# Block products in the first feed-forward as well, with w2 parts and modulation columns re-routed

## Chip, core and metric

One Trainium2 chip, and on it one core. The metric is the device time of one execution in microseconds (us); several executions are taken and their median is given.

## The reference, cut to what matters

A two-layer backbone over 512 tokens of width 1024 with 256 context tokens. Layer 0 mixes with a 2-D Fourier transform and windowed attention, layer 1 with a pooling mixer; each layer ends with a SwiGLU feed-forward of hidden width 2816. Every sub-layer is normed and modulated by shift, scale and gate columns that come from the condition `c`.

```python
def ada_mod(cond, w, b):
    m = jax.nn.silu(cond) @ w + b
    return jnp.split(m[..., None, :], 6, axis=-1)
def swiglu(h, w1, w3, w2):
    return (jax.nn.silu(h @ w1) * (h @ w3)) @ w2
...
    for layer in range(DEPTH):
        sh1, sc1, g1, sh2, sc2, g2 = ada_mod(c, ada_w[layer], ada_b[layer])
        ...
        h = h + g1 * y
        hn = modulate(rms_norm(h, norm_ffn_g[layer]), sh2, sc2)
        h = h + g2 * swiglu(hn, ffn_w1[layer], ffn_w3[layer], ffn_w2[layer])
    return rms_norm(h, final_g)
```

All of it is float32.

## The kernel before

**Layout and precision.** The stream `h` lies transposed in SBUF: 128 partitions by 8 blocks (`kt`) by 512 tokens. A float32 product is made of three TensorE passes over a high and a low part (`passes`, lines 181 to 185): w_h with the high part of the moving operand, w_l with the high part, w_h with the low part. So each weight and each activation is split first: the high part is a copy into the shorter format on ACT (`act`, line 68), the low part is source minus high part on VectorE (line 153).

**The feed-forward (`ffn`, line 1018).** The 2816 hidden channels are 22 tiles of 128, in three groups of 8, 8 and 6 (`GROUPS`). First come the normed inputs: `norm_apply` makes for each kt an `nrm_u` (VectorE, line 360), its high part `hnh` (ACT) and its low part `hnl` (VectorE, line 366). For each hidden tile, w1 and w3 products go into PSUM, `si` is the silu of the one (ACT), `av` the product with the other (VectorE), `ah` and `al` its parts. After a group come eight w2 products (`w2_ps`, one for each dt), which VectorE adds to h (line 1083) scaled by the gate column.

A *direct* tile has 48 matmuls 128x512: for each kt three passes of w1 and three of w3. Tile 0 is the *lead* (`Lead`): its product runs on the stream before the norm is known, with correction by a shift (`wb`, `sh_ps`, `z`). A *quartered* tile (`Quarters`, line 903) makes the same two products from 2x2 blocks with seven block products instead of eight (the scheme of Strassen and Winograd): 7 x 4 x 3 = 84 matmuls 128x256. For it the inputs are combined once per layer (`pieces`: `t_f` and its parts t_h, t_l on VectorE and ACT, four of them, t1 to t4), the weights of every tile are combined (`prepare`: `s_f`, four VectorE operations of 512, then split into w_h and w_l), and the outputs are combined after the products (`run`: x, y, c_q, three to five small operations). The parts of the two uncombined weights come by `low`: ACT writes the high part and its negative, and a DMA from POOL's queue adds the weight from DRAM to that negative (line 941). In `run` the products come in the order b11, t1, t2, b21, t3, b22, t4; the first use of each result bank waits until its last reader is through. `QUARTERED` says which tiles of which layer: none of layer 0, 4 to 21 of layer 1.

**Weight stream (`Stream`).** `ws` holds all units (w1, w3, w2 parts) in order of use. SP's queue loads them raw, 512 KB each, into four rotating buffers; `split` fills rotating slots for w_h and w_l, two units ahead of use.

**Modulation columns (`AdaCols`).** A `step` is one load of 512 KB (`ada_r`) and one VectorE operation over 128x1024 with an accumulator (line 222), which gives 128 columns' worth of `silu(c) @ w`. `acol1` has 88 steps; those that remain when layer 0's feed-forward begins go there, three after each tile from tile 2 on (the program's condition `l == 0 and j > 1`), and share the raw buffers with the weights.

**What sets the order.** Each engine runs its queue in order. The program is written in a natural order and a scheduler orders each engine's queue by its own estimates; `pinned` ties an instruction to its place behind the last one written for its engine; in a layer with quartered tiles PE keeps the written order (`manual_schedule`). SBUF is shared out by pools; a tile in a reused place waits for the last user of that place.

Of the kernel before, what the change touches and what calls it, by code (L numbers as in the profile page):

```python
# [16 lines left out]
P = 128  # L17
# [6 lines left out]
QUARTERED = (frozenset(), frozenset(range(4, NHID)))  # L24
NA = 17
# [6 lines left out]
def kernel(  # L32
# [47 lines left out]
    def f32(ap):  # L80
        return ap.bitcast(F32)
# [4 lines left out]
    def pick(pool, tag):  # L86
        return pb if tag == "tmp" else pool

# [37 lines left out]
    class Stream:  # L126


        def __init__(self, units, LD=4, LS=2):
            self.units, self.LD, self.LS, self.raw, self.ready, self.used = units, LD, LS, [], [], 0  # L130
            self.whole, self.slots = {i for i, u in enumerate(units) if len(u) > 2}, 0
# [23 lines left out]

        def slots_for(self, n):
            pool, t = (wp_, "") if alt["pool"] is None or self.slots % 2 == 0 else (alt["pool"], "2")
            self.slots += 1
            return [pool.tile([P, n], F32R, tag=w + t, bufs=3, name=m) for w, m in (("whi", "w_h"), ("wlo", "w_l"))]
# [44 lines left out]
    class AdaCols:  # L204


        def __init__(self, blocks):
            self.tasks = [(l, t) for l, t0 in blocks for t in range(t0, t0 + 8)]
            self.raw, self.done = [], 0

        def load(self, n):
            while len(self.raw) < min(n, len(self.tasks)):
                l, t = self.tasks[len(self.raw)]
                self.raw.append(raw_tile(1024, "ada_r"))
                nc.sync.dma_start(out=self.raw[-1], in_=adaR[48 * l + t])

        def step(self, ahead=1):
# [10 lines left out]
            self.load(self.done + ahead)  # L228

    class Norm:  # L230
# [7 lines left out]
        def add(self, kt, src):  # L238
            sq, n = self.sq, self.n
            tag, bufs = sq[:2] if kt else sq[2:]  # L240
            s = pick(self.pool, tag).tile([P, n], F32, tag=tag, bufs=bufs, name="sq")
# [136 lines left out]
    def ffn_units(l):  # L378
        u = []
        for gi, (j0, nj) in enumerate(GROUPS):  # L380
            for j in range(j0, j0 + nj):
                whole = (True,) if j in QUARTERED[l] else ()
                u += [(w1[l, j], 1024) + whole, (w3[l, j], 1024) + whole]
            u += [(w2a[l, gi, dt] if gi < 2 else w2b[l, dt], nj * P) for dt in range(KT)]
        return u
# [8 lines left out]
    with ExitStack() as es:  # L394
# [3 lines left out]
        def sl(name, n=512, dt=F32, tag="tmp", bufs=8):  # L398
            return pick(pt, tag).tile([P, n], dt, tag=tag, bufs=bufs, name=name)
# [494 lines left out]
    pq = stage.enter_context(tc.tile_pool(name="pq", bufs=1))  # L894
# [3 lines left out]
    def sf(name, n=512, dt=F32, tag="tmp", bufs=8):  # L898
        return pick(pf, tag).tile([P, n], dt, tag=tag, bufs=bufs, name=name)
# [3 lines left out]
    class Quarters:  # L903
# [79 lines left out]
        def run(self, left):  # L983
# [4 lines left out]
            x, y, si = sf("x"), sf("y"), sf("si")  # L988
            c = self.pool.tile([P, 768], F32, tag="c", bufs=1, name="c_q")
            q0, q1, q2 = [slice(256 * q, 256 * q + 256) for q in range(3)]  # L990
# [13 lines left out]
            nc.vector.tensor_tensor(c[:, q2], y[:, q0], r[3], op=ALU.add)  # L1004
# [5 lines left out]
            nc.vector.tensor_tensor(c[:, q0], x[:, q1], r[2], op=ALU.add)  # L1010
            act(si[:, q1], c[:, q0], AF.Silu)
            self.product(r[3], w["a22"], 0, "t4")
            nc.vector.tensor_tensor(c[:, q1], x[:, q1], r[3], op=ALU.add)
            av = sf("av")
            nc.vector.tensor_tensor(av, si, c[:, 256:768], op=ALU.mult)
            return av

    def ffn(l, rstd, A, lead, each=None, pool=None):
        nonlocal ss
        nrm = Norm(pf, T)  # L1020
# [17 lines left out]
        for gi, (j0, nj) in enumerate(GROUPS):  # L1038
            a = []
            for j in range(j0, j0 + nj):  # L1040
# [30 lines left out]
                if l == 0 and j > 1:  # L1071
                    for _ in range(3):
                        acol1.step()
            for dt in range(KT):
# [5 lines left out]
                for j in range(nj):  # L1080
# [3 lines left out]
                                               in1=h[:, dt, :], op0=ALU.mult, op1=ALU.add)  # L1084
                if gi == len(GROUPS) - 1:
# [10 lines left out]
    bh = pq.tile([P, 4, 536], F32R, tag="bh", bufs=1, name="bh")  # L1096
    bl = pq.tile([P, 4, 40], F32R, tag="bl", bufs=1, name="bl")
# [36 lines left out]
    nrm = ffn(0, rstd, Af, lead, pool_in)  # L1134
# [66 lines left out]
    with tc.tile_pool(name="pt8", bufs=1, reuse_waits="tile") as pt8:  # L1201
        rstd = ffn(1, rstd, Af1, lead, pool=pt8).rstd_short()
# [107 lines left out]
```

## Time and profile before

| | |
|---|---|
| median of 3 runs | 996.86 us (995.17 to 997.55) |
| the profiled execution | 996.72 us, of which the span of the profile is 995.0 us |
| granted TensorE clock | 0.994 |
| busy: PE, VectorE (DVE), ACT, POOL | 962.3, 665.6, 450.6, 58.5 us |
| layer 0's feed-forward, from its second tile on | 252.4 to 601.6 us, PE 348.82 of 349.20 busy |
| HBM read | 150.41 MB |

Rows of the profile name line, engine, operation, output and inputs with shapes. In rows of groups, "xN | busy, mean ns | idle before" gives the count, the summed time, the mean of one and the engine's idle time just ahead of them with what ended it. In rows of single instructions the first number is the start in us and the second the duration. Line L68 is the helper `act`, so ACT rows are told apart by their tiles.

### The profile page before, as it was taken

The page shows a single profiled execution, that of the slowest core. Times are in us where ns is not written, and L with a number is a line of the kernel's source. Part 1 is how long each engine was busy: PE and PEld are TensorE (multiplying, and loading weights), DVE is VectorE, ACT ScalarE, POOL GpSimd, SP SyncE. Part 2 cuts the span into 40 slices and gives each one's busy share as a digit, 9 for nine tenths or more (in the row PEclk, how much of TensorE's full clock was granted, in tenths as well). Part 3 has the DMA queues.
Part 4 walks back from the last instruction along what each step waited for, and adds up shares of the span by engine and source line. Part 5 has one row for each costly group of instructions (what it writes and reads, how often), then busy time and mean ns, then how long its engine had stood idle before and what let it go on. Part 6 is the DMA issues. An engine that isn't in the chain of part 4 may idle for free.

```text
span 995.0 us, 14007 instructions
## 1 busy us (share of the span) xinstructions
PE 962.3 (97%) x5464; PEld 804.6 (81%) x5464; DVE 665.6 (67%) x1086; ACT 450.6 (45%) x707; POOL 58.5 (6%) x63
## 2 busy tenths in 40 slices
PE   5999999998999999999999999999999999999995
PEld 3767777776888888888888888789988999889984
DVE  4678677879966546655365388998645776458644
ACT  4467666445632212223122365675533765337531
POOL 1011011002000000000000001000010110101100
PEclk9999999999999999999999999999999999999998
DMA  9931211653576546665366333136652786527602
GB/s 338 345 106 32 106 44 65 217 189 119 178 267 239 187 134 219 223 225 193 106 212 200 118 108 127 33 74 181 180 149 64 184 187 176 153 64 174 150 17 85
DMA packets 49602, 153.43 MB, mean 154 GB/s; under 512 B 6016, under 2 KB 6144, under 8 KB 49536
## 3 DMA queue, kind: packets, MB, share of 16 engines
q1 hardware_dynamic: 44352, 138.38, 41.1%
q0 software_dynamic: 5184, 14.16, 8.4%
q8 instruction: 43, 0.70, 0.3%
q14 instruction: 23, 0.19, 0.1%
HBM read 150.41 MB, written 2.10 MB: 153 GB/s over the span
## 4 chain that ended last, share of the span: by engine, by line
PE 89%; DVE 6%; ACT 3%; issue 2%; DMA 0%; DVEq 0%; SPq 0%; ACTq 0%
PE h_ps L183 15%; PE h_ps L184 15%; PE h_ps L185 15%; PE w_ps L184 8%; PE w_ps L183 8%; PE w_ps L185 8%; PE pv_ps L769 2%; PE t_ps L758 2%; PE mo_ps L183 1%; PE mo_ps L185 1%; PE mo_ps L184 1%; ACT w_h L68 1%; PE s_ps L721 1%; PE s_cx L434 1%; DVE w_l L153 1%
## 5 line engine op out<-in xcount | busy, mean ns | idle before, releaser
L68 ACT ACTIVATE w_h<-w_r 128x1024 fp32r<-128x1024 f32 (+2 forms) x158 | 148.7, 943 | 255.1 <-PE h_ps L185 115.8
L184 PE MATMUL h_ps<-hnh,w_l 128*128 128x512 f32 (+1 forms) x600 | 210.8, 351 | 0.4 <-DVE w_l L153 0.4
L183 PE MATMUL h_ps<-hnh,w_h 128*128 128x512 f32 (+1 forms) x600 | 210.9, 351 | 0.0
L185 PE MATMUL h_ps<-hnl,w_h 128*128 128x512 f32 (+1 forms) x600 | 210.7, 351 | 0.0
L153 DVE TENSOR_TENSOR w_l<-w_r,w_h 128x1024 fp32r<-128x1024 f32 (+2 forms) x122 | 137.1, 1126 | 33.6 <-ACT w_h L68 33.2
L222 DVE SCALAR_TENSOR_TENSOR ada_r<-ada_r,condB 128x1024 f32<-128x1024 f32 x80 | 97.6, 1222 | 70.2 <-DMA ada_r<-in_adaR_dram 70.1
L183 PE MATMUL w_ps<-ah,w_h 128*128 128x512 f32 x352 | 137.0, 389 | 0.0
L184 PE MATMUL w_ps<-ah,w_l 128*128 128x512 f32 x352 | 137.0, 389 | 0.0
L185 PE MATMUL w_ps<-al,w_h 128*128 128x512 f32 x352 | 137.0, 389 | 0.0
L184 PEld LDWEIGHTS h_ps<-hnh,w_l 128*128 128x128 f32 x600 | 113.6, 189 | 15.7 <-DVE w_l L153 0.8
L183 PEld LDWEIGHTS h_ps<-hnh,w_h 128*128 128x128 f32 x600 | 113.6, 189 | 15.1
L185 PEld LDWEIGHTS h_ps<-hnl,w_h 128*128 128x128 f32 x600 | 113.6, 189 | 14.9
L1083 DVE SCALAR_TENSOR_TENSOR h<-w_ps,ada,h 128x512 f32<-128x512 f32 x48 | 36.0, 750 | 91.2 <-PE w_ps L185 91.2
L183 PE MATMUL h_ps<-t_h,w_h 128*128 128x256 f32 x288 | 82.3, 286 | 1.4 <-DVE av L1060 0.9
L185 PE MATMUL h_ps<-t_l,w_h 128*128 128x256 f32 x288 | 81.6, 283 | 0.0
L184 PE MATMUL h_ps<-t_h,w_l 128*128 128x256 f32 x288 | 81.5, 283 | 0.0
L185 PEld LDWEIGHTS w_ps<-al,w_h 128*128 128x128 f32 x352 | 66.1, 188 | 13.8
L183 PEld LDWEIGHTS w_ps<-ah,w_h 128*128 128x128 f32 x352 | 66.1, 188 | 13.7
L184 PEld LDWEIGHTS w_ps<-ah,w_l 128*128 128x128 f32 x352 | 66.1, 188 | 13.4
L68 ACT ACTIVATE w_h<-s_f 128x1024 fp32r<-128x1024 f32 x36 | 38.2, 1060 | 60.5 <-PE w_ps L185 30.7
L183 PEld LDWEIGHTS h_ps<-t_h,w_h 128*128 128x128 f32 x288 | 55.2, 192 | 2.6 <-DVE c_q L1004 1.4
L184 PEld LDWEIGHTS h_ps<-t_h,w_l 128*128 128x128 f32 x288 | 55.3, 192 | 0.0
(274 smaller groups left out, 1543.9 us busy)
## 6 DMA issues: line engine op xcount, KB each, us to landing
w_r<-in_w_dram SPq DMA_DIRECT2D x88, 512.0 KB, 4.1
ada_r<-in_adaR_dram SPq DMA_DIRECT2D x80, 512.0 KB, 4.2
w_r<-in_w2a_dram SPq DMA_DIRECT2D x32, 512.0 KB, 4.4
w_l<-in_w_dram POOLq DMA_DIRECT2D x18, 512.0 KB, 5.9
ada_q<-in_adaP_dram SPq DMA_DIRECT2D x32, 256.0 KB, 5.7
w_r<-in_w2b_dram SPq DMA_DIRECT2D x16, 384.0 KB, 3.1
w_l<-in_w_dram POOLq DMA_DIRECT2D x18, 256.0 KB, 6.0
w_r<-in_wo_dram SPq DMA_DIRECT2D x16, 256.0 KB, 2.8
```

What stands on the lines that cost most here:

```text
L68: return nc.scalar.activation(out=out, in_=in_, func=func, **kw)
L153: nc.vector.tensor_tensor(lo, src, f32(hi), op=ALU.subtract)
L183: nc.tensor.matmul(acc, wh, mh, start=start, stop=False, skip_group_check=shared)
L184: nc.tensor.matmul(acc, wl, mh, start=False, stop=False, skip_group_check=shared)
L185: nc.tensor.matmul(acc, wh, ml, start=False, stop=stop, skip_group_check=shared)
L222: nc.vector.scalar_tensor_tensor(out=r, in0=r, scalar=1.0, in1=condB, op0=ALU.mult, op1=ALU.mult, accum_out=ada[l][:, t:t + 1])
L434: nc.tensor.matmul(ps[32 * g:32 * g + 32, :], condS[:, kt, :], r[:, k * n:(k + 1) * n], start=(kt < 4), stop=(kt >= 4), tile_position=(0, ...
L721: nc.tensor.matmul(sp[:, c:c + n], q, KH[kv][:, k0:k0 + n], start=True, stop=False)
L758: nc.tensor.transpose(tp[:, c * P:(c + 1) * P], Ps[c][:, n * P:(n + 1) * P], ident)
L769: nc.tensor.matmul(ops[64 * kv:64 * kv + 64, 0:256], VS[:, kbs[n], kv, :], th[:, 256 * kv:256 * kv + 256], start=(n == 0), stop=(n == N - ...
L1083: nc.vector.scalar_tensor_tensor(out=h[:, dt, :], in0=acc, scalar=ada[l][:, 40 + dt:41 + dt], in1=h[:, dt, :], op0=ALU.mult, op1=ALU.add)
```

## The change

`QUARTERED` gets the tiles 6 to 21 of layer 0 as well. Round it, memory and work are moved:

- The remaining columns: two steps after each of tiles 1 to 5 of layer 0 in the shared raw buffers; from then on two buffers of their own ("adar"), one step after each quartered tile and 11 in each w2 stage of groups 0 and 1; the last eight in layer 1's first tiles. All are pinned on VectorE.
- The w2 units of layer 0 ("alone") are no longer loaded and split: POOL's queue loads the high part itself, ACT writes its negative into the low part's place, POOL's queue adds the weight to that (`by_dma`). They are filled three units ahead instead of two.
- The temporaries of the pool `pb` go to `pt` and `pf` (six instead of eight in `pf`), `NA` is 16 instead of 17, `c_q` takes a temporary of 512, and the pool that holds the combined inputs is opened inside `ffn`, for both layers. The buffers of the pooling stage are opened ahead of the last w2 stage of layer 0.

```diff
-QUARTERED = (frozenset(), frozenset(range(4, NHID)))
-NA = 17
+QUARTERED = (frozenset(range(6, NHID)), frozenset(range(4, NHID)))
+NA = 16
...
+                if len(self.raw) in self.alone:
+                    self.raw.append(None)
+                    continue
...
-            while len(self.ready) < min(used + self.LS, len(self.units)):
+            while len(self.ready) < len(self.units):
                 k = len(self.ready)
-                if k in self.whole:
+                if k in self.whole or k >= used + self.LS + (k in self.alone):
                     break
                 self.load(k + 1)
-                self.ready.append(self.split(self.raw[k]))
+                self.ready.append(self.split(self.raw[k]) if k not in self.alone else self.by_dma(self.units[k]))
...
+        def by_dma(self, unit):
+            hi, lo = self.slots_for(unit[1])
+            nc.gpsimd.dma_start(out=hi, in_=unit[0])
+            act(lo, f32(hi), scale=-1.0)
+            nc.gpsimd.dma_start(out=lo, in_=unit[0], accum_op=ALU.add)
+            return hi, lo
...
-                self.raw.append(raw_tile(1024, "ada_r"))
+                self.raw.append(pf.tile([P, 1024], F32, tag="adar", bufs=2, name="ada_r") if self.alone
+                                else raw_tile(1024, "ada_r"))
...
-            u = pb.tile([P, n], F32, tag="tmp", bufs=8, name="nrm_u")
+            u = pool.tile([P, n], F32, tag="tmp", bufs=8, name="nrm_u")
...
-    def sf(name, n=512, dt=F32, tag="tmp", bufs=8):
-        return pick(pf, tag).tile([P, n], dt, tag=tag, bufs=bufs, name=name)
+    def sf(name, n=512, dt=F32, tag="tmp", bufs=6):
+        return pf.tile([P, n], dt, tag=tag, bufs=bufs, name=name)
...
-            c = self.pool.tile([P, 768], F32, tag="c", bufs=1, name="c_q")
+            x, y, si, c = sf("x"), sf("y"), sf("si"), sf("c_q")
...
-    def ffn(l, rstd, A, lead, each=None, pool=None):
+    def ffn(l, rstd, A, lead, each=None, then=None):
+        phase = ExitStack()
+        pool = phase.enter_context(tc.tile_pool(name="pt8", bufs=1, reuse_waits="tile"))
...
-                if l == 0 and j > 1:
-                    for _ in range(3):
-                        acol1.step()
+                if j > 0:
+                    acol1.alone = l == 1 or j + 1 >= quartered[0]
+                    for _ in range(2 if (j == 6 if l else j < quartered[0]) else 1):
+                        if l or acol1.done < 48:
+                            pinned(DVE, acol1.step)
+            if gi == len(GROUPS) - 1:
+                phase.close()
+                if then:
+                    then()
...
+                if l == 0 and gi < 2:
+                    for n in range(2 if dt % 3 == 2 or dt == 0 else 1):
+                        pinned(DVE, acol1.step)
```

Where the order of the queues moves, first VectorE at the start of layer 0's feed-forward, before (`wb` belongs to the lead, `nrm_u` and `hnl` to the normed inputs):

```order
L153 TENSOR_TENSOR w_l<-w_r,w_h 128x1024
L315 SCALAR_TENSOR_TENSOR wb<-w_r,ada_106,wb 128x128
L360 SCALAR_TENSOR_TENSOR nrm_u<-h,Af_2364,bc_ps 128x512
L315 SCALAR_TENSOR_TENSOR wb<-w_r,ada_106,wb 128x128
L360 SCALAR_TENSOR_TENSOR nrm_u<-h,Af_2364,bc_ps 128x512
L315 SCALAR_TENSOR_TENSOR wb<-w_r,ada_106,wb 128x128
L366 SCALAR_TENSOR_TENSOR hnl<-nrm_u,ada_106,hnh 128x512
```

The first two nrm_u stand between the last wb. The same place on VectorE after the change:

```order
L163 TENSOR_TENSOR w_l<-w_r,w_h 128x1024
L326 SCALAR_TENSOR_TENSOR wb<-w_r,ada_106,wb 128x128 x3
L371 SCALAR_TENSOR_TENSOR nrm_u<-h,Af_2364,bc_ps 128x512
L163 TENSOR_TENSOR w_l<-w_r,w_h 128x1024
L371 SCALAR_TENSOR_TENSOR nrm_u<-h,Af_2364,bc_ps 128x512
L377 SCALAR_TENSOR_TENSOR hnl<-nrm_u,ada_106,hnh 128x512
```

All wb now stand ahead of the first nrm_u, which in the built program waits for the last `sh_ps` matmul, the end of the lead product; sixteen norm operations follow it.

VectorE after the change from tile 3's last column steps to tile 5's av (`s_f` are the combined weights of the tiles 6 and 7; the second av is tile 5's):

```order
L233 SCALAR_TENSOR_TENSOR ada_r,ada_106<-ada_r,condB 128x1024 x2
L163 TENSOR_TENSOR w_l<-w_r,w_h 128x1024
L963 TENSOR_TENSOR s_f<-w_r 128x512
L968 TENSOR_TENSOR s_f<-w_r 128x512
L1072 TENSOR_TENSOR av<-si,h_ps 128x512
...
L163 TENSOR_TENSOR w_l<-s_f,w_h 128x1024
L233 SCALAR_TENSOR_TENSOR ada_r,ada_107<-ada_r,condB 128x1024 x2
L963 TENSOR_TENSOR s_f<-w_r 128x512
L968 TENSOR_TENSOR s_f<-w_r 128x512
L1072 TENSOR_TENSOR av<-si,h_ps 128x512
```

Before, such av had only w_l and column steps around them; now the column steps and s_f of the quartered tiles stand ahead of both av. In SP's queue the raw loads of tile 6 wait for the buffers that the two steps of the first row read.

ACT after the change, from the x of group 0's last tile (tile 7) to that tile's ah; `w_l<-w_h` of 1024 are the negatives of w2 parts, each behind a plain transfer of POOL's queue:

```order
L68 ACTIVATE x<-h_ps 128x256
L68 ACTIVATE w_l<-w_h 128x1024
L68 ACTIVATE si<-h_ps 128x256
L68 ACTIVATE w_l<-w_h 128x1024
L68 ACTIVATE si<-y 128x256
L68 ACTIVATE w_l<-w_h 128x1024
L68 ACTIVATE w_h<-w_r 128x512
L68 ACTIVATE ah<-av 128x512
```

Three such passes stand ahead of the ah that the w2 products need, where before the ACT queue had splits of loaded weights (`w_h<-w_r`) between si and ah. Two more stand ahead of the x of that tile.

More of the change, by code (lines that the diff above doesn't have):

```diff
@@ L84, in big @@
         return pb.tile([P, 4, T], F32R, tag="b8", bufs=4, name=name)
-    def pick(pool, tag):
-        return pb if tag == "tmp" else pool
     cond_sb = cp.tile([P, KT, 2], F32, name="cond_sb")
@@ L130, in __init__ @@
             self.units, self.LD, self.LS, self.raw, self.ready, self.used = units, LD, LS, [], [], 0
-            self.whole, self.slots = {i for i, u in enumerate(units) if len(u) > 2}, 0
+            self.whole, self.slots = {i for i, u in enumerate(units) if u[2:] == ("whole",)}, 0
+            self.alone = {i for i, u in enumerate(units) if u[2:] == ("alone",)}
         def load(self, n):
@@ L154, in split @@
             return hi, lo
[L156 to L159, printed above, removed]
         def take(self, n):
@@ L179, in peek, with slots_for @@
             return self.raw[self.used + n]
+        def slots_for(self, n):
+            pool, t = (wp_, "") if alt["pool"] is None or self.slots % 2 == 0 else (alt["pool"], "2")
+            self.slots += 1
+            return [pool.tile([P, n], F32R, tag=w + t, bufs=3, name=m) for w, m in (("whi", "w_h"), ("wlo", "w_l"))]
     def passes(acc, w, m, start, stop, shared=False):
@@ L208, in __init__ @@
             self.tasks = [(l, t) for l, t0 in blocks for t in range(t0, t0 + 8)]
-            self.raw, self.done = [], 0
+            self.raw, self.done, self.alone = [], 0, False
         def load(self, n):
@@ L227, in step @@
                 nc.vector.tensor_tensor(ada[l][:, c], ada[l][:, c], adaB_sb[:, l, c], op=ALU.add)
-            self.load(self.done + ahead)
+            self.load(self.done + ahead + self.alone)
     class Norm:
@@ L240, in add @@
             tag, bufs = sq[:2] if kt else sq[2:]
-            s = pick(self.pool, tag).tile([P, n], F32, tag=tag, bufs=bufs, name="sq")
+            s = self.pool.tile([P, n], F32, tag=tag, bufs=bufs, name="sq")
             if kt in self.pool_at:
@@ L381, in ffn_units @@
             for j in range(j0, j0 + nj):
-                whole = (True,) if j in QUARTERED[l] else ()
+                whole = ("whole",) if j in QUARTERED[l] else ()
                 u += [(w1[l, j], 1024) + whole, (w3[l, j], 1024) + whole]
-            u += [(w2a[l, gi, dt] if gi < 2 else w2b[l, dt], nj * P) for dt in range(KT)]
+            u += [(w2a[l, gi, dt] if gi < 2 else w2b[l, dt], nj * P) + (() if l else ("alone",)) for dt in range(KT)]
         return u
@@ L1065, in ffn @@
                 if quartered and j < quartered[0]:
-                    for _ in range((0, 1, 2, 1)[j]):
+                    for _ in range((0, 1, 2, 1, 0, 0)[j]):
                         next(pieces)
@@ L1095, with pool_stage @@
     xs, A1, PX = [], [], []
-    bh = pq.tile([P, 4, 536], F32R, tag="bh", bufs=1, name="bh")
-    bl = pq.tile([P, 4, 40], F32R, tag="bl", bufs=1, name="bl")
+    def pool_stage():
+        nonlocal pq, bh, bl
+        pq = stage.enter_context(tc.tile_pool(name="pq", bufs=1, reuse_waits="tile"))
+        bh = pq.tile([P, 4, 536], F32R, tag="bh", bufs=1, name="bh")
+        bl = pq.tile([P, 4, 40], F32R, tag="bl", bufs=1, name="bl")
     def pool_band_load(g):
@@ L1132, in pool_in @@
             pool_shift(kt - 5)
-    nrm = ffn(0, rstd, Af, lead, pool_in)
+    nrm = ffn(0, rstd, Af, lead, pool_in, pool_stage)
     rs_c = nrm.rstd_cols()
@@ L1200 @@
     stage.close()
-    with tc.tile_pool(name="pt8", bufs=1, reuse_waits="tile") as pt8:
-        rstd = ffn(1, rstd, Af1, lead, pool=pt8).rstd_short()
+    rstd = ffn(1, rstd, Af1, lead).rstd_short()
     wide.close()
```

19 lines of the change are left out of this document (9 added, 10 removed).

## The prediction, made before the changed kernel was run

> **What bounds the kernel now.** I read the page's first part and chain, then windows of two stretches, then groups by shape, then single rows where layer 0's feed-forward starts and where layer 1 enters its quartered tiles.
>
> ```profile
> span 995.0 us, 14007 instructions
> PE 962.3 (97%) x5464; PEld 804.6 (81%) x5464; DVE 665.6 (67%) x1086; ACT 450.6 (45%) x707; POOL 58.5 (6%) x63
> ...
> PE 89%; DVE 6%; ACT 3%; issue 2%; DMA 0%; DVEq 0%; SPq 0%; ACTq 0%
> ```
>
> TensorE is the bound: less matmul time is less time, as long as nothing makes PE wait. The two windows below are layer 0's feed-forward from its second tile to its end, with direct tiles only, and a piece of layer 1's quartered tiles (columns: busy us and count of PE, PEld, DVE, ACT, POOL; granted clock; DMA share; GB/s).
>
> ```profile
> core 0: us, PE busy (x) PEld busy (x) DVE busy (x) ACT busy (x) POOL busy (x), PEclk, DMA share, GB/s
> 252.40:601.60 349.20, 348.82 (x1542) 288.73 (x1541) 213.27 (x313) 110.66 (x142) 0.00 (x0) 1.00 0.55 187
> 784.00:831.00 47.00, 47.00 (x393) 46.95 (x392) 35.60 (x57) 32.53 (x47) 7.85 (x9) 1.00 0.79 184
> ```
>
> Layer 0 has no PE idle to win back (0.38 of 349.20 us), so only fewer or shorter matmuls help, and any new wait is a full loss. A 512-wide matmul takes 349.20/1542 = 0.2265 us; a direct tile has 48: 10.87 us. For a quartered tile I take the distance between two POOL issues four tiles apart; the second fence has their durations and what they wait for.
>
> ```profile
> 785.40 0.87 POOL L941 DMA_DIRECT2D w_l<-in_w_dram  x1 [2.48 <-PE h_ps L185]
> 795.48 0.86 POOL L941 DMA_DIRECT2D w_l<-in_w_dram  x1 [2.33 <-PE h_ps L185]
> ...
> 825.83 0.87 POOL L941 DMA_DIRECT2D w_l<-in_w_dram  x1 [2.31 <-PE h_ps L185]
> ```
> ```profile
> L941 POOL DMA_DIRECT2D w_l<-in_w_dram x36: 856/866/1011, 637.7 to 930.6; - x36
> ...
> DMA to landing us min/median/max: 4.0/5.9/8.3
> ```
>
> The first two are 10.08 apart, the four tiles 40.43, so 10.08 to 10.11 a tile, or 0.12 us for each of 84 matmuls 256 wide, with VectorE busy 35.60 of 47.00 us.
>
> **The gain.** Sixteen tiles of layer 0 go from 10.87 to 10.08: 16 x 0.79 = 12.6 us (12.2 at 10.11). PE's order has nothing else taken out.
>
> **The start of layer 0.** Rows of VectorE there, before:
>
> ```profile
> 245.38 0.74 DVE L360 SCALAR_TENSOR_TENSOR nrm_u<-h,Af,bc_ps 128x512 f32<-128x512 f32 x1
> ...
> 251.19 0.74 DVE L366 SCALAR_TENSOR_TENSOR hnl<-nrm_u,ada,hnh 128x512 fp32r<-128x512 f32 x1
> 252.68 1.23 DVE L153 TENSOR_TENSOR w_l<-w_r,w_h 128x1024 fp32r<-128x1024 f32 x1 [0.74 <-ACT w_h L68]
> ...
> 257.23 0.75 DVE L366 SCALAR_TENSOR_TENSOR hnl<-nrm_u,ada,hnh 128x512 fp32r<-128x512 f32 x1
> 257.89 1.22 DVE L153 TENSOR_TENSOR w_l<-w_r,w_h 128x1024 fp32r<-128x1024 f32 x1
> 259.05 0.75 DVE L366 SCALAR_TENSOR_TENSOR hnl<-nrm_u,ada,hnh 128x512 fp32r<-128x512 f32 x1
> 259.71 0.68 DVE L344 TENSOR_TENSOR z<-h_ps,rb 128x512 f32<-128x512 f32 x1
> 260.31 1.22 DVE L153 TENSOR_TENSOR w_l<-w_r,w_h 128x1024 fp32r<-128x1024 f32 x1
> ```
>
> The starts give the pitches: nrm_u and hnl 0.66, w_l 1.16, a 512-wide two-input operation 0.60. Nine of the sixteen norm operations run beside the lead product (tile 0's), which ends at about 252.4. After the change nrm_u lies in space that was freed just before, and its first write waits for the last sh_ps matmul, the end of that product. So from 252.6 come 16 x 0.66 = 10.6 plus two or three w_l in between, 2.3 to 3.5: the last hnl ends at about 265.8 instead of 259.8. Tile 1 needs it 1.36 us (six matmuls) before its end, so it ends at about 267 instead of the 264 that the lead, a 0.4 to 0.8 us wait and 48 matmuls give now. Cost 2.8 us (2.0 to 3.5; the low end if the two splits slip behind the norm).
>
> **The entry into the quartered tiles.** VectorE's groups of the stretches that hold such work, from two answers (layer 1's stage, and 252 to 420 for the column step):
>
> ```profile
> L153 DVE TENSOR_TENSOR w_l<-s_f,w_h 128x1024 fp32r<-128x1024 f32 x24 | 29.4, 1224 | 9.8 <-ACT w_h L68 9.7
> ...
> L952 DVE TENSOR_TENSOR s_f<-w_r 128x512 f32<-128x512 f32 x13 | 9.0, 692 | 5.2 <-DMA w_r<-in_w_dram 4.9
> ...
> L933 DVE TENSOR_TENSOR t_l<-t_f,t_h 128x1024 fp32r<-128x1024 f32 x4 | 4.9, 1222 | 0.0
> ```
> ```profile
> L222 DVE SCALAR_TENSOR_TENSOR ada_r<-ada_r,condB 128x1024 f32<-128x1024 f32 x34 | 41.4, 1223 | 36.3 <-DMA ada_r<-in_adaR_dram 36.3
> ...
> L222 DVE DVE_READ_ACCUMULATOR ada_r<-ada_r,condB 128x1 f32 x34 | 2.8, 83 | 0.0
> ```
> ```profile
> q1 hardware_dynamic: 44352, 138.38, 41.1%
> q0 software_dynamic: 5184, 14.16, 8.4%
> ...
> w_r<-in_w_dram SPq DMA_DIRECT2D x88, 512.0 KB, 4.1
> ada_r<-in_adaR_dram SPq DMA_DIRECT2D x80, 512.0 KB, 4.2
> ```
> ```profile
> 662.12 1.79 DVE L928 SCALAR_TENSOR_TENSOR t_f<-nrm_u,ada,t_f 128x256 f32<-128x256 f32 x4
> 663.83 1.22 DVE L933 TENSOR_TENSOR t_l<-t_f,t_h 128x1024 fp32r<-128x1024 f32 x1
> ```
>
> From the first nrm_u to the av of tile 5, VectorE's new order has 16 norm operations (x 0.66 = 10.6), 11 w_l and 4 t_l (x 1.16 = 17.4), 19 two-input operations z, av, al, s_f (x 0.61 = 11.6), 16 t_f (1.71 for four: 6.8) and 10 column steps (1.25 with the accumulator read: 12.5): 58.9 us. Tile 6's second product t1 uses banks that tile 5's av must read first, as in layer 1:
>
> ```profile
> 677.36 0.28 PE L183 MATMUL h_ps<-hnh,w_h 128*128 128x256 f32 x1
> ...
> 679.11 0.68 DVE L1060 TENSOR_TENSOR av<-si,h_ps 128x512 f32<-128x512 f32 x1
> ...
> 679.85 0.39 PE L183 MATMUL h_ps<-t_h,w_h 128*128 128x256 f32 x1 [0.90 <-DVE av L1060]
> ```
>
> There av ran 1.2 us late. In layer 0 it is due at 267 + 4 x 10.87 + 1.44 = 311.9; VectorE from 252.6 without any wait gets there at 311.5. So each idle us of VectorE counts. The loads of tile 6's raw weights take over buffers that column steps must release first; the second is issued behind the second step of tile 3 and lands 4.1 later, with one w_l (1.16) to fill the time: 3 us idle. ACT's in-order queue (two w_h, t_h and si ahead of av) adds 0.5 to 1.5; tile 4's second w_l comes 0.8 late, which PE waits for too; and c_q, two s_f behind its due place in tile 6, 0.5. Cost 4.8 us (1.5 if these waits overlap with those of the start; 7 if the loads land in 6 rather than 4.1). Without the column steps (12.5 us) this stretch would be covered, as layer 1's nearly is.
>
> **w2 parts by DMA.** 24 units lose a VectorE split (24 x 1.16 = 28 us, hidden now beside PE: worth nothing there) and keep one ACT pass of the same 1.06. New are 48 POOL issues of 0.87 us; POOL has room. But ACT, in order, now waits for a plain POOL transfer ahead of work that PE needs. A plain POOL transfer is not in the trace; I bound it by 4.1 (SP's load) and 5.9 (POOL's accumulate) and take 5, in the middle. With the tile before the last of a group at 0: the first high part is issued after t2 (4.3 + 0.87) and the second after b21, landing at 10.7 to 12.5; then two passes of 1.06, two of 0.63, ah 0.63 and x 0.38 are through at 14.1 to 15.9, and the last tile's b21 needs x at 14.4. Further on two more high parts land at 21.1 to 23.7, and ah of the last tile follows at 23.4 to 26.0; the w2 product needs it at 20.16 + 21 x 0.2265 = 24.9 in groups of eight, 23.6 in the last. So 0 to 2.6 us for each of three groups; I take 0.8 each, 2.5 in all (0 to 7). [...]
>
> **The rest.** Column steps in the w2 stages: 11 in 43.5 us (eight units of 5.44); two buffers of 1.25 + 4.2 to 6 each give a step every 2.7 to 3.6 us, enough for 1.4 a unit; 0 to 1. Steady quartered tiles: one step of 1.25 on top of 35.6/47 x 10.08 = 7.6 makes 8.9 of 10.08, hidden but thin; 0 to 2. Eight steps in layer 1's first tiles and the pool stage's buffers: 0 to 1, and below nothing by 0.5, since layer 0's tail has no steps. Together 0.7.
>
> Sum: -12.6 + 2.8 + 4.8 + 2.5 + 0.7 = -1.8. The profiled execution took 996.72 us (span 995.0 and 1.7 around it), 0.14 under the median; 996.86 - 1.8 = 995.
>
> **Rivals.** (1) The gain stays. VectorE is idle in layer 0 for lack of loads (36.3 us in the group row), so a tighter order may catch up and only the start and half of the entry count: -12.6 + 2.8 + 2.4 = -7.4, 989.5 (986 to 992.4). For it: no PE idle in layer 0 today. Against: the 58.9 us of work in 59.3.
> (2) Slower: the DMA engines fill up in groups 0 and 1. By the queue rows the hardware queue took 0.411 x 995/138.38 = 2.96 us for a MB and POOL's accumulates 0.084 x 995/14.16 = 5.9: 1.55 and 3.1 us for 512 KB. A quartered tile takes 0.79 x 10.08 = 8.0 us plus a column 1.55; eight of them, eight w2 units (1.55 + 3.1 each) and 11 columns make 76 + 37 + 17 = 130 us of the 124 that group 1 lasts. It decides once that exceeds the PE time; then the missing 6 us in group 1 and about as much in group 0's short stretch (81 against 70) come back as late columns that hold VectorE, h and PE: +6 to +10, 1001 to 1005; where the queues overlap better, 997 to 1000. Against it: packet times contain waiting, so the sum is too high, and the w2 parts are issued units ahead.
> [...]
>
> **The numbers.** About 0.3%, 3 us, is what a measurement tells from no change. Forecast (losses of 8.1 to 12.7: 992.4 to 997) 0.40; rival 1 0.27; rival 2 0.30; rival 3 0.03. Faster (under 993.9): all of rival 1 and a third of the forecast, 0.40. Slower (over 999.8): most of rival 2 (0.22) and of rival 3 (0.02), 0.24. Same: 0.36. The range 987 to 1004 leaves out a tenth at each end; the forecast's own is 992.4 to 997.
>
> **What would show it.** In the profile after: quartered tiles of layer 0 at 10.1 us; nrm_u starting after 252 with PE idle 2 to 3.5 us in tile 1; one wait of t1 on av near 312 of 2 to 5 us; ACT w_l rows of the w2 units waiting for DMAs ahead of x and ah, with PE idle under 2.6 us a group; DMA share of group 1 under 0.95. I am wrong if PE is idle in the w2 stages behind h, if the entry shows no wait (rival 1), or if the plain POOL transfers take over 6 us.

## The result, and the profile after

The changed kernel takes 1067.85 us (median of 4 runs, 1066.61 to 1069.42) against 996.59 for the kernel before (4 runs): a ratio of 1.0717, interval 1.0697 to 1.0737. The forecast was 995, in a range of 987 to 1004. The profiled execution took 1066.61, its span is 1064.8, 69.8 us longer than before.

The same parts of the page as were shown of before:

```profile
span 1064.8 us, 15550 instructions
PE 981.3 (92%) x6040; PEld 843.5 (79%) x6040; DVE 718.5 (67%) x1227; ACT 513.3 (48%) x807; POOL 120.2 (11%) x143
...
q1 hardware_dynamic: 40896, 126.84, 35.5%
q0 software_dynamic: 16704, 49.81, 23.9%
...
PE 60%; DVE 14%; issue 10%; DMA 8%; ACT 4%; POOL 2%; DVEq 0%; SPq 0%; POOLq 0%; ACTq 0%
```

PE was 89% of the chain and is 60%; VectorE, ACT and DMA now stand in it with 26%. PE's idle time rose from 995.0 - 962.3 = 32.7 to 83.5 us: 50.8 more. Its busy time should have fallen by the 12.6 us of the block products to 949.7, and is 981.3: 31.6 more, though the matmuls are the planned ones. So 50.8 us are waits and about 31.6 are slower matmuls; less the 12.6, that is the 69.8.

What PE waited for from the start of layer 0's feed-forward to the middle of layer 1's start (columns: total us, times, longest):

```profile
PE w_ps L193 <- DVE h L1101: 12.1, 3, 6.9
PE w_ps L193 <- ACT ah L68: 11.6, 3, 5.1
PE h_ps L193 <- DVE y L1010: 9.2, 2, 5.5
PE nrm_ps L272 <- DVE sq L263: 5.2, 1, 5.2
PE h_ps L193 <- DVE av L1072: 4.3, 1, 4.3
PE h_ps L193 <- ACT x L68: 2.8, 2, 2.2
PE h_ps L193 <- ACT hnh L68: 1.8, 1, 1.8
```

The forecast priced the rows av and hnh, and x and ah at 2.5 us in all. The rows h, y and sq were not in its sum; only its second rival names h. Where the slower matmuls come from shows in PE's rows behind one of these waits:

```profile
388.09 0.79 PE L193 MATMUL w_ps<-ah,w_h 128*128 128x512 f32 x1 [4.63 <-DVE h L1101]
388.68 0.63 PE L194 MATMUL w_ps<-ah,w_l 128*128 128x512 f32 x1
389.11 0.63 PE L195 MATMUL w_ps<-al,w_h 128*128 128x512 f32 x1
...
393.37 0.63 PE L193 MATMUL w_ps<-ah,w_h 128*128 128x512 f32 x1
393.80 0.50 PE L194 MATMUL w_ps<-ah,w_l 128*128 128x512 f32 x1
394.14 0.39 PE L195 MATMUL w_ps<-al,w_h 128*128 128x512 f32 x1
```

After 4.63 us without work the matmuls start 0.43 us apart, and from 394.14 on 0.23: for 6 us PE runs at half speed, and the wait costs 2.9 us more than it lasts. Over the rest of the program from the feed-forward on, matmul starts that are farther apart than at full speed, waits left out, add up to about 38 us by the start times in the trace, against about 7 before.

The way to the wait of 4.63 us, the longest in group 0's w2 stage, goes through the queues of four engines. First what SP's queue waited for between 340 and 400 us, then rows of ACT and POOL, then of SP and of VectorE:

```profile
SPq L226 <- DVE ada_r L233: 46.1, 9, 14.3
SPq L139 <- ACT w_h L68: 11.1, 1, 11.1
```
```profile
362.85 1.06 ACT L68 ACTIVATE w_l<-w_h 128x1024 fp32r<-128x1024 f32 x1 [13.49 <-DMA w_h<-in_w2a_dram]
371.17 1.06 ACT L68 ACTIVATE w_l<-w_h 128x1024 fp32r<-128x1024 f32 x1 [7.26 <-DMA w_h<-in_w2a_dram]
372.14 1.04 ACT L68 ACTIVATE w_h<-w_r 128x1024 fp32r<-128x1024 f32 x1
```
```profile
364.32 0.86 POOL L155 DMA_DIRECT2D w_l<-in_w2a_dram  x1 [11.14 <-ACT w_l L68]
364.93 0.82 POOL L153 DMA_DIRECT2D w_h<-in_w2a_dram  x1
```
```profile
373.21 0.33 SPq L139 DMA_DIRECT2D w_r<-in_w_dram  x1
373.63 0.89 SPq L226 DMA_DIRECT2D ada_r<-in_adaR_dram  x2
```
```profile
383.55 1.23 DVE L233 SCALAR_TENSOR_TENSOR ada_r<-ada_r,condB 128x1024 f32<-128x1024 f32 x1 [15.61 <-DMA ada_r<-in_adaR_dram]
...
387.29 0.75 DVE L1101 SCALAR_TENSOR_TENSOR h<-w_ps,ada,h 128x512 f32<-128x512 f32 x1
```

ACT stands still for 13.49 us and then for 7.26, each time until the high part of a w2 unit has landed. The second of these parts was issued only at 364.93, behind an accumulating transfer that waits in POOL's queue for the first pass of ACT. The split behind the second pass in ACT's queue is the one that frees a raw weight buffer. SP's queue waits 11.1 us for that buffer with the loads of two columns behind it; the first of these has landed ten us later; VectorE stands still for 15.61 us at the column step, with the update of h behind it; and PE, which has three banks, waits 4.63 for h.

### The profile page after: what moved, and what is told of

Read it like the earlier page. It is cut to its first block, busy times and chain, and to the rows that moved or that the text cites. A ratio compares the mean times of both kernels' runs of the same rounds, so it can differ in the third digit from the quotient of the medians.

```text
span 1064.8 us, 15550 instructions
## 1 busy us (share of the span) xinstructions
PE 981.3 (92%) x6040; PEld 843.5 (79%) x6040; DVE 718.5 (67%) x1227; ACT 513.3 (48%) x807; POOL 120.2 (11%) x143
## 4 chain that ended last, share of the span: by engine, by line
PE 60%; DVE 14%; issue 10%; DMA 8%; ACT 4%; POOL 2%; DVEq 0%; SPq 0%; POOLq 0%; ACTq 0%
PE h_ps L193 10%; PE h_ps L194 10%; PE h_ps L195 10%; PE w_ps L193 4%; PE w_ps L194 4%; PE w_ps L195 4%; DMA w_r<-in_w_dram 3%; DVE w_l L163 2%; DMA ada_r<-in_adaR_dram 2%; PE pv_ps L780 2%; DMA w_h<-in_w2a_dram 2%; ACT w_h L68 2%; DVE ada_r L233 2%; PE t_ps L769 1%; PE mo_ps L193 1%
## 5 line engine op out<-in xcount | busy, mean ns | idle before, releaser
L193 PE MATMUL h_ps<-hnh,w_h 128*128 128x256 f32 (+1 forms) x536 | 168.8, 315 | 14.0 <-DVE y L1010 9.2
L68 ACT ACTIVATE w_h<-w_r 128x1024 fp32r<-128x1024 f32 (+2 forms) x134 | 118.1, 882 | 118.9 <-PE h_ps L195 37.8
L195 PE MATMUL h_ps<-hnl,w_h 128*128 128x256 f32 (+1 forms) x536 | 168.2, 314 | 0.8 <-DVE hnl L377 0.8
L194 PE MATMUL h_ps<-hnh,w_l 128*128 128x256 f32 (+1 forms) x536 | 167.8, 313 | 0.0
L193 PE MATMUL h_ps<-t_h,w_h 128*128 128x256 f32 x544 | 157.6, 290 | 8.4 <-DVE av L1072 7.7
L193 PE MATMUL w_ps<-ah,w_h 128*128 128x512 f32 x352 | 142.1, 404 | 23.7 <-DVE h L1101 12.1
L194 PE MATMUL h_ps<-t_h,w_l 128*128 128x256 f32 x544 | 156.4, 288 | 0.0
L195 PE MATMUL h_ps<-t_l,w_h 128*128 128x256 f32 x544 | 156.2, 287 | 0.0
L68 ACT ACTIVATE w_l<-w_h 128x1024 fp32r<-128x1024 f32 (+2 forms) x92 | 80.9, 881 | 100.3 <-DMA w_h<-in_w2a_dram 71.9
L952 POOL DMA_DIRECT2D w_l<-in_w_dram x68 | 59.3, 871 | 512.9 <-ACT w_l L68 463.1
L195 PEld LDWEIGHTS h_ps<-t_l,w_h 128*128 128x128 f32 x544 | 106.9, 196 | 0.0
L163 DVE TENSOR_TENSOR w_l<-s_f,w_h 128x1024 fp32r<-128x1024 f32 x68 | 83.1, 1224 | 18.0 <-ACT w_h L68 17.5
```

The source lines that it names most:

```text
L68: return nc.scalar.activation(out=out, in_=in_, func=func, **kw)
L163: nc.vector.tensor_tensor(lo, src, f32(hi), op=ALU.subtract)
L193: nc.tensor.matmul(acc, wh, mh, start=start, stop=False, skip_group_check=shared)
L194: nc.tensor.matmul(acc, wl, mh, start=False, stop=False, skip_group_check=shared)
L195: nc.tensor.matmul(acc, wh, ml, start=False, stop=stop, skip_group_check=shared)
L952: nc.gpsimd.dma_start(out=lo, in_=dram, accum_op=ALU.add)
```

## The experiments

Each was run once if nothing else is said. Gains and losses are counted from the changed kernel's 1067.85, which was not run again beside them; the kernel before took 997.3 us beside e1 to e4, 995.9 beside e5 to e8, 998.4 beside e9 to e11 and 998.6 beside e12, so a difference of 2 or 3 us between runs of different sets says nothing.

**e1: w2 units split as before.**

```diff
-            u += [(w2a[l, gi, dt] if gi < 2 else w2b[l, dt], nj * P) + (() if l else ("alone",)) for dt in range(KT)]
+            u += [(w2a[l, gi, dt] if gi < 2 else w2b[l, dt], nj * P) + () for dt in range(KT)]
```

> Edit: the w2 units of layer 0 are loaded by SP and split on ACT and VectorE as before the change; everything else stays as changed. Theory Q (queues in order: ACT waits for a plain POOL transfer of a w2 part ahead of si, x, ah and sq, and SP's raw load waits for ACT with column loads behind it): the waits of PE at the three ends of groups (6.5, 9.6, 7.6 us with the half-speed matmuls behind them) and at the end of layer 0 (7.4) go, about 31 us, to 1037; if the column loads no longer get stuck either, another 15 to 29, to 1008 to 1022. Rival C (column steps alone, the w2 transfers innocent): the w2 stages keep their waits of 4.8 and 7.0 us on h, and the time stays over 1050.

Measured 1016.99, 50.9 less. PE's waits in the same stretch:

```profile
PE h_ps L193 <- DVE av L1072: 7.7, 2, 3.9
PE h_ps L193 <- DVE y L1010: 7.2, 2, 4.9
PE h_ps L193 <- DVE c_q L1014: 3.0, 4, 1.5
```

The rows h, ah, x and sq are gone; y is left. So the w2 parts by DMA cost 51 of the 71 us (with their filling three units ahead, which goes with them), and they made h late, not only ah and x. Rival C, the columns alone, falls.

**e2: no column steps in the w2 stages.**

```diff
-                if l == 0 and gi < 2:
-                    for n in range(2 if dt % 3 == 2 or dt == 0 else 1):
-                        pinned(DVE, acol1.step)
```

> Edit: the 22 column steps in the w2 stages of groups 0 and 1 of layer 0 are left out with their loads (part of the modulation of layer 1 is not computed); everything else stays as changed. Rival C: the waits on h and y in these stages (4.8 and 3.9, 7.0 and 5.7 us, with the half-speed matmuls 7.7 + 5.8 + 8.6 + 7.4 = 29.5) go, 1038, and the ends of groups stay. Theory Q: the same 29 us at most, since a stuck SP queue then holds no column; if the s_f loads behind the stuck raw load hold VectorE as well, only 10 to 15 go, 1053 to 1058. If the DMA engines were simply full, the ends of groups shrink too and the time goes under 1030.

Measured 1036.72, 31.1 less. The waits on h and y of the two w2 stages are gone; those on ah (12.6 us in all, the longest 6.3) and sq (5.2) stay, as both theories allowed. The steps are counted through, so most of the 22 are not left out, as the expectation has it, but run later: 14 of them in layer 1's later tiles, eight not at all (72 steps and 74 loads instead of 80 and 80). From layer 1's first t1 product to the end the kernel takes 317.6 us, the changed one 317.7, so the later steps cost nothing that shows there. That the waits on ah did not shrink although the loads were gone from these stages spoke against full DMA engines; e6 and e9 show that this was concluded too early.

**e3: another rule for the space.**

```diff
-    pf = ctx.enter_context(tc.tile_pool(name="pf", bufs=2))
+    pf = ctx.enter_context(tc.tile_pool(name="pf", bufs=2, reuse_waits="tile"))
```

> Edit: one word, the pool of the feed-forwards waits tile by tile for the space that it takes over (reuse_waits), everything else stays as changed. Theory S (the first nrm_u waits for the whole lead product since its space counts as one): the waits of 2.0 and 1.0 us at the start and the 3 us of half-speed matmuls behind them go, and VectorE enters tile 6 earlier, so that the 4.4 us there shrink: 1067.9 - 5 to 12 = 1056 to 1063. Rival: the first nrm_u is held by the very tile that it replaces, nothing changes, 1067.

Measured 1067.95: nothing. VectorE's rows there:

```profile
246.75 0.74 DVE L371 SCALAR_TENSOR_TENSOR nrm_u<-h,Af,bc_ps 128x512 f32<-128x512 f32 x1
253.27 1.23 DVE L163 TENSOR_TENSOR w_l<-w_r,w_h 128x1024 fp32r<-128x1024 f32 x1 [5.78 <-ACT w_h L68]
```

The first nrm_u no longer waits (it starts at 246.75 instead of 251.75), but the w_l behind it does, for ACT's w_h, whose slot the lead product still reads. The theory was right on the first wait and wrong on its worth: the queue had a second one of nearly the same length (5.78 us after 6.85), and tile 2 starts at 268.05 us instead of 268.29.

**e4: no block products in layer 0**, all else as changed.

```diff
-QUARTERED = (frozenset(range(6, NHID)), frozenset(range(4, NHID)))
+QUARTERED = (frozenset(), frozenset(range(4, NHID)))
```

> Edit: layer 0 has no quartered tiles, everything else stays as changed (columns with two buffers, w2 parts by DMA, pools). If the block products' own VectorE, ACT and DMA work is what crowds the queues, the time falls to the old one, 995 to 1005. Theory Q: the w2 parts and the columns do it by themselves; then the ends of groups and the w2 stages keep a good part of their waits and the time is 1015 to 1045, although 12.6 us of matmul time are added back.

Measured 1010.40, between the two expectations. With direct tiles the w2 parts by DMA are almost harmless: one wait of 3.3 us on h, none on ah or x. (PE's order in layer 0 is the scheduler's here, as before the change.) It is the meeting of the two that costs. Late landing alone does not: here are the ends of the tiles of groups 0 and 1 (PE, PEld, DVE, ACT, POOL busy, clock, DMA share, GB/s) and the plain transfers of the high parts:

```profile
310.00:350.00 40.00, 40.00 (x178) 33.11 (x177) 14.58 (x23) 10.05 (x12) 9.33 (x13) 1.00 0.92 249
455.00:490.00 35.00, 35.00 (x156) 29.00 (x155) 12.91 (x22) 7.76 (x9) 7.72 (x11) 1.00 0.92 237
```
```profile
DMA to landing us min/median/max: 3.4/6.8/10.3
```

The DMA engines are nearly full (0.92) and the median is 6.8 us, which e6 below shows for the changed kernel too, but PE does not wait once (busy 40.00 of 40.00 and 35.00 of 35.00 us). In the changed kernel the same lateness meets queues in which the x, si, s_f and raw loads of quartered tiles stand behind it. Which of these matters most, and whether the two accumulating transfers that each quartered tile adds on POOL's queue do, no run separates. What stays above the old time is the start (2.6 us of waits), the wait on h and 4.1 on av at layer 1's entry (0.90 before).

**e5: e1 and e2 together.**

```diff
-            u += [(w2a[l, gi, dt] if gi < 2 else w2b[l, dt], nj * P) + (() if l else ("alone",)) for dt in range(KT)]
+            u += [(w2a[l, gi, dt] if gi < 2 else w2b[l, dt], nj * P) + () for dt in range(KT)]
...
-                    for n in range(2 if dt % 3 == 2 or dt == 0 else 1):
-                        pinned(DVE, acol1.step)
```

> Edit: both of the earlier edits, the w2 units of layer 0 loaded and split as before the change, and the 22 column steps of the w2 stages left out with their loads (part of layer 1's modulation is not computed). Left of the change in layer 0: the block products, the new places, the ten column steps ahead of tile 6 and one a tile behind. If the two causes are separate, the gains add: 1067.9 - 50.9 - 31.1 = 986. If they are one chain that either edit cuts, the second adds only what the first left in these stages (waits of 2.5, 1.0, 1.6, 5.0 and their half-speed matmuls, 13 us): 1003 to 1005.

Measured 1007.19: 60.7 less, not 82. The two causes are one chain that either edit cuts in part, as rows of ACT, SP and VectorE above suggested. (Expected for one chain were 1003 to 1005. As in e2, 14 of the column steps run later.)

**e6: no accumulating transfer for w2 parts.**

```diff
             act(lo, f32(hi), scale=-1.0)
-            nc.gpsimd.dma_start(out=lo, in_=unit[0], accum_op=ALU.add)
```

> Edit: the second POOL transfer of each w2 part of layer 0 (the accumulating one) is left out, so that the low part is only the negative of the high one (w2 products are then not the right ones); the high transfers, the ACT passes that wait for them and all else stay as changed. Theory D (the DMA engines are full at the ends of groups, so high parts take 7 to 10 us to land): with 24 accumulating transfers of about 3 us of all engines fewer, high parts land in 4 to 6 us, the waits for ah and x (0.8 + 3.7, 2.4 + 3.2, 5.3 us) shrink by half or more, and the time is 1025 to 1045. Theory Q (queues in order, slots freed late by PE): landing hardly matters, 1058 to 1068.

Measured 1021.12, 46.7 less, a little below the range of theory D. How long the plain high transfers took to land, in the changed kernel and here:

```profile
DMA to landing us min/median/max: 4.2/6.8/13.0
```
```profile
DMA to landing us min/median/max: 3.2/5.2/6.9
```

The waits on h are gone here, those on ah are down from 11.6 to 1.8 us; y keeps 8.5 us.

**e9: the accumulating transfer kept in its place, 16 columns of it.**

```diff
-            nc.gpsimd.dma_start(out=lo, in_=unit[0], accum_op=ALU.add)
+            nc.gpsimd.dma_start(out=lo[:, 0:16], in_=unit[0][:, 0:16], accum_op=ALU.add)
```

> Edit: the accumulating POOL transfer of each w2 part of layer 0 is kept in its place in the queue, with all that it waits for and all that waits for it, but adds only 16 of the 1024 or 768 columns (the w2 products are then not the right ones): 8 KB instead of 512. If its bytes (the load on the DMA engines) made the high parts late: as with the transfer left out, 1021 (1018 to 1030). If its place in POOL's queue did (the high parts that are issued behind it wait until ACT has made the negative): the time stays near the changed kernel's, 1050 to 1066. In between if both do.

Measured 1030.10. The bytes of the 24 accumulating transfers account for 37.8 us and their place in POOL's queue for the other 9.0, give or take the 2 or 3 us between sets. The plain transfers' landing, with the bytes gone, and windows over the end of group 0's tiles and of group 1's (PE, PEld, DVE, ACT, POOL busy, clock, DMA share, GB/s), changed kernel first, then e9:

```profile
DMA to landing us min/median/max: 3.4/5.6/7.9
```
```profile
320.00:360.00 40.00, 35.80 (x213) 31.87 (x213) 17.01 (x30) 11.45 (x18) 10.90 (x15) 0.93 1.01 257
465.00:500.00 35.00, 29.49 (x184) 26.56 (x184) 13.77 (x27) 11.57 (x18) 10.93 (x16) 0.90 0.97 246
```
```profile
320.00:360.00 40.00, 38.06 (x221) 33.94 (x221) 18.33 (x33) 12.48 (x19) 12.28 (x17) 0.91 0.79 208
465.00:500.00 35.00, 33.09 (x172) 28.39 (x171) 15.37 (x28) 13.48 (x19) 10.90 (x15) 0.95 0.70 200
```

In the changed kernel the DMA engines are busy all the time there (share 1.01 and 0.97), at 246 to 257 GB/s; without the bytes they have a quarter to spare (0.79 and 0.70), and PE works 2.3 and 3.6 us more of the same stretch. (The second stretch is the same by the clock but not by the work: e9 is 9 us further on there.)

**e7: column steps without their loads.** A step in the w2 stages reads the column that is there.

```diff
+                if self.hold:
+                    self.raw.append(self.raw[-1])
+                    continue
...
+                acol1.hold = l == 0 and gi < 2 and dt < KT - 1
```

> Edit: the column steps of the w2 stages of groups 0 and 1 still run on VectorE, but read the columns that are there already; their loads are left out (columns of layer 1 are then not the right ones). If the wait for loads behind SP's stuck raw load is what holds h and y: as with the steps left out altogether, 1037 (1034 to 1043). If it is VectorE's time for the steps (22 x 1.3 us), the waits stay: 1060 to 1068.

Measured 1038.48, nearly as without the steps (1036.72, in another set), with all 80 steps run and 20 loads fewer. VectorE's 22 x 1.3 us cost 2 or 3 us at most; it is the waits for loads.

**e10: e1, and columns loaded from POOL's queue.**

```diff
-                nc.sync.dma_start(out=self.raw[-1], in_=adaR[48 * l + t])
+                (nc.gpsimd if self.alone else nc.sync).dma_start(out=self.raw[-1], in_=adaR[48 * l + t])
```

> Edit: w2 units of layer 0 loaded by SP and split as before the change (1017 by itself), and the loads of the columns with buffers of their own issued from POOL's queue instead of SP's. If a raw weight load that stands in SP's queue ahead of column loads and waits for its buffer is what makes columns late: the waits on y in the tiles 8 and 16 (2.5 and 5.0 us, 2.7 more at half speed) go and the time is 1006 to 1010. If the columns are late because two buffers are too few or the DMA engines are full: 1014 to 1025, later than from SP since a transfer from POOL takes longer to land.

Measured 1006.41, 10.6 below e1; y's two waits of 7.2 us became one of 1.7. With w2 split as before, then, the columns were late because they stood in SP's queue behind a raw weight load, not because two buffers were too few. For the changed kernel itself the rows of SP and VectorE above say the same; this edit was not run on it.

**e8: no column steps ahead of tile 6.**

```diff
-                if j > 0:
+                if j > 0 and (l or j + 1 >= quartered[0]):
```

> Edit: the ten column steps ahead of tile 6 of layer 0 are left out with their loads, all but one after tile 5 (part of the modulation is not computed); everything else stays as changed. Theory E (VectorE has 58.9 us of work for 59.3 there, and the raw loads wait for column buffers): t1's wait of 4.4 us on av and the half-speed matmuls behind it (2.1) go or fall under 1 us, and 10 x 1.25 us less work ahead lets tile 7 and the first w2 stage start on time: 1058 to 1062. Rival: the wait is set by the chain of weights for tile 6 (loads, s_f, w_h, w_l) whatever the columns do: 1066 to 1068.

Measured 1060.66, 7.2 less. PE's wait at tile 6, changed kernel and here:

```profile
PE h_ps L193 <- DVE av L1072: 4.3, 1, 4.3
```
```profile
PE h_ps L193 <- DVE av L1074: 0.9, 1, 0.9
```

The wait is 3.4 us shorter; in the changed kernel the matmuls behind it are 0.21 us apart instead of 0.12 from 317.67 to 322.34 us, which costs 2.1. If these go too, 5.5 of the 7.2 us are named. The columns were what made VectorE late, as forecast. (Here too the steps are counted through: all 80 run, nine of those ahead of tile 6 now in layer 1's later tiles.)

**e11 and e12: versions that could be better.** Both load and split w2 as before the change. e11 starts the block products at tile 12, with all columns ahead of it; e12 at tile 8, where the weights can be combined in group 0's w2 stage, with columns from POOL's queue and none in layer 1.

```diff
-QUARTERED = (frozenset(range(6, NHID)), frozenset(range(4, NHID)))
+QUARTERED = (frozenset(range(12, NHID)), frozenset(range(4, NHID)))
...
+                if l == 0 and 1 < j < quartered[0]:
+                    for _ in range(4):
+                        acol1.step()
...
+                if l == 0 and gi == 0:
+                    for _ in range(2):
+                        acol1.step()
```

> A version that could be better than both: layer 0's block products only in tiles 12 to 21, w2 units loaded and split as before the change, all remaining columns ahead of tile 12 in the shared buffers (four after each of tiles 2 to 11, two for each w2 unit of group 0), none later. By the waits seen so far: 10 x 0.79 = 7.9 us less matmul time, against 3.4 more at the start, 1 to 3 at tile 12 and about 3 in small waits of c_q and y: 994 to 997 against 996.6. If the columns crowd the direct tiles (4 x 1.25 + 3.5 us of VectorE in 10.87, six loads of 512 KB): 1000 or more.

Measured 1012.59 (4 runs), ratio 1.0141, interval 1.0121 to 1.0161: not the 994 to 997 expected but the other branch, 1000 or more. The entry moved with its wait and grew:

```profile
438.44 0.58 PE L193 MATMUL h_ps<-t_h,w_h 128*128 128x256 f32 x1 [8.99 <-DVE av L1072]
```

In the last 20 us ahead of it VectorE waits 2.17, 0.99 and 2.82 us for loads of columns, with the s_f and the av of the entry behind them.

```diff
-QUARTERED = (frozenset(range(6, NHID)), frozenset(range(4, NHID)))
+QUARTERED = (frozenset(range(8, NHID)), frozenset(range(4, NHID)))
...
-                    if j + 1 == quartered[0]:
+                    if j + 1 == quartered[0] < j0 + nj:
...
-                    for _ in range(2 if (j == 6 if l else j < quartered[0]) else 1):
-                        if l or acol1.done < 48:
+                    for _ in range(3 if j < quartered[0] else 1):
+                        if l == 0:
```

> A version drawn from the runs: layer 0's block products only in tiles 8 to 21 (the first combined weights are then made in group 0's w2 stage, where VectorE has room), w2 units loaded and split as before the change, columns with own buffers loaded from POOL's queue, three after each of tiles 1 to 7, the rest in the w2 stages and quartered tiles, none in layer 1. By the waits seen: 14 x 0.79 = 11.1 us less matmul time; the wait of t1 at tile 6 (4.2 + 2.0) is gone, the one at layer 1's entry back to 1.1 + 2.1; left are 3.4 at the start and small waits of 4 to 6: 992 to 996 against 996.6. If entering after a w2 stage meets late loads as tile 12 did (9.2 + 4.4): 1000 to 1006.

Measured 1006.7 (10 runs, 1000.06 to 1010.33), ratio 1.0075, interval 1.0051 to 1.0099: just over the other branch of the expectation, 1000 to 1006. The longest of PE's waits, in a run of 1006.64:

```profile
PE h_ps L193 <- DVE y L1010: 3.3, 2, 2.6
PE h_ps L193 <- DVE c_q L1014: 2.6, 4, 0.9
PE w_ps L193 <- ACT ah L68: 2.6, 1, 2.6
```

No wait is over 2.65 us, and they still eat the 11.1 us: from layer 0's feed-forward on PE is idle for 19.7 us against 5.9 before, and the granted clock over the span is 0.983 to 0.991 in the ten runs, against 0.991 to 0.995 in those of the kernel before beside them. Neither version beats the kernel before; no run did.

## Why the prediction was wrong

**The gain** was right: PE's counts are those of 16 quartered tiles, and a stretch without waits (420 to 460 us) has 333 matmuls in 40.00 us, 0.12 each.

**The start, 2.8 us.** The first link was right: nrm_u started at 251.75 behind sh_ps. But the step has PE held at the end of tile 1 by the last hnl. That one has ended at 264.7, two us before it is needed, and holds nothing; PE is held at the tile's beginning, 1.8 us for hnh and 0.8 for hnl, and then runs at half speed for 2.9 us more. Tile 2 starts at 268.29 instead of 264.06: 4.2 us, above the step's 2.0 to 3.5. And e3 shows that the step named one of two causes: the w_l behind nrm_u would have waited nearly as long.

**The entry into tile 6, 4.8 us.** Right in place and cause: VectorE stood for the raw load of tile 6 where the step has 3 us,

```profile
303.42 0.69 DVE L963 TENSOR_TENSOR s_f<-w_r 128x512 f32<-128x512 f32 x1 [3.69 <-DMA w_r<-in_w_dram]
```

and PE waited 4.3 us on av. The size was nearly right: with 2.1 at half speed, 7.2 by e8.

**w2 parts by DMA, 2.5 us.** This is the step that failed most: 50.9 by e1. The high part was taken to land in 5 us, between two rows of a kernel in which POOL's queue was busy for 8.4% of the engines' time; it took 6.8 in the median and up to 13.0, over the 6 that the prediction gave as a sign of being wrong. Its own accumulating partners fill the DMA engines where it is needed (share 1.01); without their bytes the median is 5.6 (e9). By the bounds of the prediction each us more of landing moved x and ah by one us; at 13 that is already 7 a group. But lateness was not all of it, as e4 shows with the same median and hardly a wait. The larger error is that only x and ah were followed. Behind the same ACT pass stood the split that frees SP's raw buffer, behind that the columns, and behind these h and y: 12.1 and 9.2 us of waits that the sum does not have.

**"The rest", 0.7 us.** Here the column steps of the w2 stages were priced at 0 to 1. Taking them out of these stages was worth 31.1 us (e2), and still 9.8 with w2 split as before (e5 against e1). The step every 2.7 to 3.6 us that two buffers give counted buffers and landing, and left out SP's queue, in which a column load stands behind raw loads. The row of 15.61 us and e10 (10.6 us from another queue alone) show it. The prediction followed ACT's queue operation by operation, but not SP's in the w2 stages.

**Rival 2**, full DMA engines in groups 0 and 1, named the right places (h and PE held by late columns) and was priced at 6 to 10 us. Its sum over a whole group, 130 us of transfers for 124 of time, is not what happened: from 403 to 545 us, group 1, the DMA share is 0.86, under the 0.95 that the prediction set as a sign, and the engines are full only where tiles end and w2 parts begin (1.01 and 0.97). For group 0 its 81 against 70 does not come out of its own terms either, which give some 73 against 64. And it counted the missing time once, where every late transfer stops an in-order queue, which holds others.

**Rival 3**, longer POOL issues at 0.03, is shown by no run: in the changed kernel those for the w2 parts took 530 to 887 ns (plain) and 855 to 1161 ns (accumulating), against 856 to 1011 ns for the accumulating ones before.

**No price for half speed.** Every PE wait was counted as long as it lasts. About 30 us of the 71 are matmuls at half speed behind waits. No row of the trace of before shows it in these stages: its granted clock is 1.00 from 240 to 700 us, and behind the wait of 0.90 us at layer 1's entry, which the prediction quotes, the matmuls start 0.12 us apart.

What stays open: the 8 to 10 us between e10 (1006.4) and the old time, and the 12.6 of the gain that are eaten as well. Of the 9.6 us between the spans, 6.4 lie behind layer 0's last w2 product (400.2 us to the end, 393.8 before). That is for the most part the entry into layer 1's quartered tiles: e12, which has no columns there, waits 0.9 us on av where e10 waits 4.0, and takes 395.4. In layer 0 the start and the entry into tile 6 (4.1 us on av) must make up most of it, but no run removed the start.

## What to carry to other kernels

When work is moved from a busy engine to DMAs, add up the transfer time of the stretch where it lands, not of the whole kernel, and take landing times from rows with that load. Then follow every in-order queue behind the waiting instruction one step further than the engine that is the bound: here the costly chain was POOL's transfer, ACT's pass, SP's raw load, the column, h. And price a new wait of some us on a busy TensorE higher than it lasts: here 50.8 us of waits brought some 31 us of matmuls at half speed with them.

## What the runs showed of the hardware that was not expected

After a wait TensorE often ran at half speed (0.43 instead of 0.23 us for 512 columns). In the trace of the changed kernel, from 250 to 760 us, the granted clock is 0.50 in five stretches of 3.41 us, seven of 6.83 and one of 13.66. Windows behind the wait of 4.63 us (columns as above; the clock is the third number from the end):

```profile
387.20:390.60 3.40, 2.51 (x6) 2.03 (x7) 3.37 (x6) 1.06 (x1) 0.00 (x0) 0.50 0.44 136
390.60:394.00 3.40, 3.40 (x9) 2.63 (x9) 3.40 (x6) 0.00 (x0) 0.00 (x0) 0.50 0.79 231
394.00:397.40 3.40, 3.40 (x20) 2.95 (x20) 1.25 (x3) 0.77 (x1) 0.00 (x0) 1.00 1.00 353
```

In the same trace and time each of PE's nine waits of 3.45 us and more (the longest 6.86) had such a stretch, which began during the wait or up to 1.7 us behind it, and so had the three of 1.83, 2.19 and 2.99 us. Behind waits of 0.65 us (at 333.58) and 0.59 us (at 641.41) the clock is 1.00, as it is behind the one of 0.90 us in the trace of before; yet one stretch, at 687.56, has only waits of 0.49 and 0.78 us close ahead of it. So the wait's length alone did not decide. In e11 the matmuls behind the wait of 8.99 us start 0.21 us apart, those ahead of it 0.12 (256 columns). The stretch shown lasts 6.83 us, from 387.19 to 394.02; PE is busy for 2.51 of 3.40 us in its first half and for all 3.40 in its second. The granted clock over the whole span fell from 0.994 to 0.957.

The accumulating transfers took about twice as long for a MB as plain loads. In e1, where POOL's queue has no others, 26.74 MB of them took 15.8% of the 16 engines' span of 1015.2 us, 6.0 us for a MB, while SP's plain loads took 41.4% for 138.38 MB, 3.0 us. Both are sums of packet times, which vary for one size: plain packets of 4096 bytes took 156 to 1660 ns in the trace of before, 159 in the median. Taking the bytes of 24 of them, 11.3 MB, out of the changed kernel made it 37.8 us faster (e9). Where they were under way in the changed kernel the DMA engines were full (share 1.01 and 0.97) at 246 to 257 GB/s, while the first slice of the kernel's span, with plain loads, moves 339 GB/s.
